# Two chunks of an MLP down-projection as seven block products in place of eight (Strassen), in a two-layer encoder on one core

## The chip, the cores and the metric

The kernel runs on one core of one Trainium2 chip. The metric is the device time of one execution, in microseconds (us): 2254.66 us, the median of 3 runs (2254.27 to 2255.26). The engines are named as in the profile: PE (matmuls), PEld (PE's weight loads), DVE (VectorE), ACT (ScalarE), POOL (GpSimd) and SP, whose queue starts the weight loads.

## The reference, cut to what matters

Two layers, each an attention mixer and a gated MLP, all in float32, with 256 tokens, a model width of 2048 and an MLP width of 5632:

```
def conv_ffn(h, w_up, conv_w, conv_b, w_down):
    u = h @ w_up                      # 256 x 2048 by 2048 x 11264
    u = depthwise conv of width 3 over positions, + conv_b
    gate, val = jnp.split(u, 2, axis=-1)
    return (jax.nn.silu(gate) * val) @ w_down     # 256 x 5632 by 5632 x 2048
...
for i in range(2):
    h = h + mixer_i(rms_norm(h, mix_norm[i]))     # grouped-query attention, then dilated windows
    h = h + conv_ffn(rms_norm(h, ffn_norm[i]), w_up[i], ...)
return rms_norm(h, final_norm)
```

## The kernel before

**Matmuls in three parts.** PE multiplies in a rounded float32 form, so every operand is split into a rounded high part and the rest. A product is three matmuls into one PSUM bank: high by high, high by low, low by high (lines 115 to 117).

**A feed.** `feed` (line 97) takes one chunk of 512 rows of a weight matrix and one block of 512 columns. SP loads it in two pieces of 128 x 1024 (512 KB each) into `raw` buffers, of which there are 4 (NRAW). ACT writes the high part `wh` (line 127), DVE the low part `wl` (line 128); there are 4 buffers of each (NHL). Both are issued under a priority that is raised by AHEAD = 60 instructions. PE then runs 24 matmuls: 2 token blocks (m) x 4 row blocks (kt) x 3. Two banks, `accs[0]` and `accs[1]`, hold the 128 + 128 tokens by 512 columns.

**Order.** The program is written out in Python and placed by a scheduler that takes, on each engine, the instruction with the best priority whose inputs and buffers are there. Side work is written as generators: `pending` ones move by one piece at every odd row block of a feed, `beside` ones at every even one, and `drain` writes out all that is left. A piece's place in the text gives its priority; it may run earlier when it is ready.

**The MLP.** `ffn` (line 362) runs in two halves of the MLP width: 6 chunks, then 5 (HALVES). In each half the up-projection makes a gate block and a value block per chunk; each is evacuated by ACT with the row scale (`stg`, line 359), turned by DVE and POOL (`turned`, lines 401 to 407, 16 POOL copies into a tile `u`), convolved by ACT (line 388) and DVE (line 396), and gate and value are multiplied on POOL (line 422). `act_split` (line 436) rounds the product into the left operands of the down-projection (`slots`, the tiles `a`). These steps run one or two chunks behind PE. After the last chunk, `flush` does the rest beside the first feeds of the down-projection.

**The down-projection.** It multiplies the half's chunks with `w_down`, in four column blocks n = 0 to 3, and adds to the residual `h`. Columns 0 and 1 run together (`project2`): all chunks but the last for n = 0, the same for n = 1, and then the last chunk, which is ready last, for both. Columns 2 and 3 follow one by one (`project`; the very last by `project_last`, which ends with the final norm and the output). `done` adds a finished block to `h`, two DVE operations of 128 x 512 (line 331 or 487). In the second half of layer 0 it also starts the transposes for the next mixer; in the second half of layer 1 it squares on ACT (line 488) and multiplies by the final gain on POOL (line 489).

PSUM has eight banks: four of tag `acc` for the projections, four of tag `ps` for everything else.

## Time and profile before

| what | value |
|---|---|
| median of 3 runs | 2254.66 us (2254.27 to 2255.26) |
| span of the profiled execution, first to last instruction | 2253.4 us |
| own time of the profiled execution | not given apart from its span; the runs' median is 1.3 us more |
| matmuls, weight loads | 10089 each |
| busy: PE, DVE, ACT, POOL | 2240.8, 1605.8, 1216.2, 760.4 us |
| wl splits of 128 x 1024 on DVE | 788, mean 1.27 us |
| wh splits of 128 x 1024 on ACT | 788, mean 1.06 us |
| moved by DMA | 439.56 MB, 195 GB/s |

A line of the profile names the source line, engine and operation, the tile written and the tiles read with their shape, and how often it ran; then the busy time with the mean of one in ns, and the idle time of the engine just before with what ended it. Lines in order of time begin with the start and the length in us; a bracket at the end holds the idle time ahead of the instruction and who ended it. Matmuls overlap each other, so that their lengths do not add up. Windows give, for a stretch of the span, its length, the busy time of PE, PEld, DVE, ACT and POOL with the number of instructions, the granted clock, and DMA's share and rate.

### The profile page before, as it was taken

What the parts mean: (1) busy time and instruction counts of PE and PEld (TensorE: products, weight loads), DVE (VectorE), ACT (ScalarE), POOL (GpSimd) and SP (SyncE); (2) the same over time, 40 slices, a digit from 0 to 9 for tenths busy, and PEclk for the clock granted to TensorE, in tenths of its full rate; (3) what the DMA queues carried; (4) which work ended last, traced back from release to release, by engine and by line L of the source; (5) the groups of instructions that cost most, each with busy time, mean ns of one, the idle gap of its engine ahead of it and who ended that gap; (6) DMA issues with size and microseconds to landing.
All of it is one profiled execution on the core that took longest, in us unless ns stands there. A gap on an engine that the chain in (4) does not pass through costs nothing.

```text
span 2253.4 us, 28552 instructions
## 1 busy us (share of the span) xinstructions
PE 2240.8 (99%) x10089; PEld 1860.1 (83%) x10089; DVE 1605.8 (71%) x2137; ACT 1216.2 (54%) x1691; POOL 760.4 (34%) x999
## 2 busy tenths in 40 slices
PE   9999999999999999999999999999999999999998
PEld 7888888888888888888888888888888888888887
DVE  6877967776546777878876877676777764576765
ACT  7676556555345655555454554445655543465653
POOL 2342165663006554010052007002665600256530
PEclk9999999999999999999999999999999999999999
DMA  8565665655555565565566555566555555555554
GB/s 302 191 222 172 203 201 190 195 193 195 194 193 192 194 193 188 191 215 195 184 191 195 180 187 175 180 201 211 195 193 193 193 196 192 193 195 194 191 196 150
DMA packets 125871, 439.56 MB, mean 195 GB/s; under 512 B 14232, under 2 KB 18072, under 8 KB 125600
## 3 DMA queue, kind: packets, MB, share of 16 engines
q1 hardware_dynamic: 123056, 429.05, 57.0%
q0 software_dynamic: 2384, 8.39, 1.5%
q8 instruction: 79, 1.29, 0.2%
q14 instruction: 64, 0.52, 0.1%
q10 hardware_dynamic: 288, 0.30, 0.0%
HBM read 432.34 MB, written 5.34 MB: 194 GB/s over the span
## 4 chain that ended last, share of the span: by engine, by line
PE 96%; DVE 2%; DMA 1%; issue 1%; POOL 1%; ACT 0%; SPq 0%; DVEq 0%; POOLq 0%; ACTq 0%
PE acc L116 31%; PE acc L115 31%; PE acc L117 31%; DVE wl L128 1%; DMA raw<-in_w_b_dram 1%; DVE tT L268 1%; PE ps L225 0%; PE ps L224 0%; PE ps L223 0%; PE ps L1031 0%; PE ps L221 0%; DMA raw<-in_w_a_dram 0%; ACT wh L127 0%; POOL wide L263 0%; POOL t L704 0%
## 5 line engine op out<-in xcount | busy, mean ns | idle before, releaser
L128 DVE TENSOR_TENSOR wl<-raw,wh 128x1024 fp32r<-128x1024 f32 (+1 forms) x804 | 1010.0, 1260 | 521.2 <-ACT wh L127 518.1
L127 ACT ACTIVATE wh<-raw 128x1024 fp32r<-128x1024 f32 (+1 forms) x804 | 840.8, 1050 | 800.7 <-PE acc L117 714.8
L115 PE MATMUL acc<-wh,xh 128*128 128x512 f32 x2176 | 848.7, 390 | 0.7 <-ACT wh L127 0.7
L116 PE MATMUL acc<-wl,xh 128*128 128x512 f32 x2176 | 847.6, 390 | 0.3 <-DVE wl L128 0.2
L117 PE MATMUL acc<-wh,xh 128*128 128x512 f32 x2176 | 847.3, 389 | 0.0
L406 POOL COPY u<-quad 32x256 f32<-32x256 f32 x704 | 489.4, 695 | 539.9 <-DVE quad L259 512.1
L117 PEld LDWEIGHTS acc<-wh,xh 128*128 128x128 f32 x2176 | 408.6, 188 | 85.5
L115 PEld LDWEIGHTS acc<-wh,xh 128*128 128x128 f32 x2176 | 408.8, 188 | 84.8 <-ACT wh L127 1.1
L116 PEld LDWEIGHTS acc<-wl,xh 128*128 128x128 f32 x2176 | 408.8, 188 | 84.5 <-DVE wl L128 1.4
L115 PE MATMUL acc<-wh,a 128*128 128x512 f32 x1008 | 392.8, 390 | 0.0
L116 PE MATMUL acc<-wl,a 128*128 128x512 f32 x1008 | 392.3, 389 | 0.0
L117 PE MATMUL acc<-wh,a 128*128 128x512 f32 x1008 | 392.2, 389 | 0.0
L117 PEld LDWEIGHTS acc<-wh,a 128*128 128x128 f32 x1008 | 189.2, 188 | 39.5 <-DVE a L210 0.2
L116 PEld LDWEIGHTS acc<-wl,a 128*128 128x128 f32 x1008 | 189.3, 188 | 39.0
L115 PEld LDWEIGHTS acc<-wh,a 128*128 128x128 f32 x1008 | 189.3, 188 | 38.6
L263 POOL COPY wide<-quad 32x256 f32<-32x256 f32 x165 | 107.2, 650 | 170.1 <-DVE quad L259 162.9
L422 POOL TENSOR_TENSOR cv<-cg,cv 128x1024 f32<-128x1024 f32 x22 | 71.1, 3232 | 135.7 <-DVE cv L396 135.7
L359 ACT ACTIVATE stg<-acc,rstd 128x512 f32<-128x512 f32 x122 | 82.9, 685 | 31.7 <-PE acc L117 31.7
L396 DVE SCALAR_TENSOR_TENSOR cg<-u,cw,cg 128x256 f32<-128x256 f32 x176 | 82.3, 511 | 4.5 <-ACT cg L388 4.5
L396 DVE SCALAR_TENSOR_TENSOR cv<-u,cw,cv 128x256 f32<-128x256 f32 x176 | 74.3, 479 | 15.5 <-ACT cv L388 15.3
L259 DVE STREAM_TRANSPOSE quad<-stg 128x512 f32<-128x512 f32 x88 | 59.4, 699 | 10.3 <-ACT stg L359 10.3
L268 DVE STREAM_TRANSPOSE tT<-h 32x256 f32<-32x256 f32 x144 | 62.8, 436 | 2.7
(172 smaller groups left out, 1037.0 us busy)
## 6 DMA issues: line engine op xcount, KB each, us to landing
raw<-in_w_up_dram SPq DMA_DIRECT2D x352, 512.0 KB, 4.5
raw<-in_w_down_dram SPq DMA_DIRECT2D x176, 512.0 KB, 4.2
raw<-in_w_b_dram SPq DMA_DIRECT2D x144, 512.0 KB, 4.4
raw<-in_w_bo_dram SPq DMA_DIRECT2D x48, 512.0 KB, 3.7
raw<-in_w_a_dram SPq DMA_DIRECT2D x40, 512.0 KB, 4.7
raw<-in_w_ao_dram SPq DMA_DIRECT2D x32, 512.0 KB, 4.0
raw<-in_w_a_dram SPq DMA_DIRECT2D x16, 256.0 KB, 5.8
there<-quad POOLq DMA_DIRECT2D x6, 512.0 KB, 3.2
```

Of the source, the lines that this page charges most:

```text
L115: nc.tensor.matmul(accs[m], xh[:, c], wh[:, j, :], start=st, stop=False)
L116: nc.tensor.matmul(accs[m], xh[:, c], wl[:, j, :], start=False, stop=False)
L117: nc.tensor.matmul(accs[m], xl[:, c], wh[:, j, :], start=False, stop=sp)
L127: nc.scalar.activation(wh[:, c], r[:, c], AF.Copy)
L128: nc.vector.tensor_tensor(wl[:, c], r[:, c], wh[:, c].bitcast(F32), ALU.subtract)
L259: nc.vector.transpose(quad[:, :, at, :], src.rearrange("p (x c t) -> p c x t", c=4, t=32))
L263: nc.gpsimd.tensor_copy(o[32 * c:32 * c + 32, :, 32 * q:32 * q + 32], quad[32 * q:32 * q + 32, c])
L268: nc.vector.transpose(o[cols].rearrange("p a (m t) -> p a m t", m=2)[:, :, :, rows], s[rows].rearrange("p m (a c) -> p a m c", c=P)[:, :, ...
L359: nc.scalar.activation(o[:, m, :], accs[m], AF.Copy, scale=rstd[:, m:m + 1])
L396: nc.vector.scalar_tensor_tensor(cj, halves(flat[:, j, o:o + NT])[:, ::-1], tap(n, j, i), cj, ALU.mult, ALU.add)
L406: nc.gpsimd.tensor_copy(u[32 * c:32 * c + 32, :, :, 32 * q:32 * q + 32], quad[32 * q:32 * q + 32, c].rearrange("p (j m) t -> p j m t", m=2))
L422: made.append(nc.gpsimd.tensor_tensor(cv, cg, cv, ALU.mult).ins)
```

## The change

In three of the four halves (both of layer 1, the first of layer 0) chunks 2 and 3 of the down-projection become *fast units*. A fast unit takes one chunk and two column blocks at once, as a 2 x 2 by 2 x 2 block product: the left matrix is cut into 2 token blocks x 2 halves of the chunk's rows, the weights into 2 halves of the rows x 2 column blocks. It makes seven block products in place of eight, each 2 row blocks x 3 matmuls, into seven banks; with the banks of the plain chunks eight are in use (`fast_accs`).

- `fast_unit` loads the four weight blocks b11, b12, b21, b22 (128 x 1024 each). DVE makes the four sums t1, b12, t2, t4, three of them in the tiles `u` and one in place, at a priority raised by 120. All seven right operands are split by ACT and DVE as in a feed.
- `combined` takes the place of `act_split` for these chunks: four differences of left blocks on DVE, and splits of those and of the blocks that are used as they are.
- `fold` adds the shared products to `h` after a pair's last fast unit: one ACT copy and eight DVE operations of 128 x 512, in four pieces beside the feeds.
- `pair` runs two column blocks together in a written order of plain feeds and fast units, in place of `project2` and `project`. Ahead of a fast unit it writes out all pending work.
- The last value block of a half is turned by ACT in place of POOL, and its product with the gate is made by DVE in place of POOL, in all four halves.
- Two more `raw` buffers come from the MLP's own pool: every third load takes one of them.
- Some tiles move: the final gain is loaded in four pieces into the tiles of the up-projection's operands, the bias lines use tiles of the left operands, the transposes use `cg` and `cv`, and a constant that nothing read is gone.

The order of the chunks, with f2 and f3 for the fast units and a plain chunk once for each of its two columns: in first halves 0 0 1 1 f2 4 4 f3 5 5 for columns 0-1 and 0 0 f2 1 1 f3 4 4 5 5 for columns 2-3; in the second half of layer 1 0 0 1 f2 1 f3 4 4, and 0 f2 1 f3 4 for columns 2-3 (the plain chunks of column 3 follow in `project_last`).

The core of the diff (left out: the moves of tiles to other tags, the bias lines and the gain's pieces):

```diff
-    def feed(accs, lhs, kg, wap, first, last, by_m=False, pieces=1, mid=None):
+    extra, count = [None], [0]
+
+    def raw_tile():
+        count[0] += 1
+        if extra[0] and count[0] % 3 == 0:
+            return extra[0].tile([P, 2, 512], F32, tag="raw2", name=nm("raw"), bufs=2)
+        return spool.tile([P, 2, 512], F32, tag="raw", name=nm("raw"), bufs=NRAW)
+
+    def feed(accs, lhs, kg, wap, first, last, by_m=False, pieces=1, mid=None, begun=()):
...
         raws, w = [], 2048 // pieces
         for i in range(max(pieces, 2)):
             if pieces < 4 or i % 2 == 0:
-                raws.append(spool.tile([P, 2, 512], F32, tag="raw", name=nm("raw"), bufs=NRAW))
+                raws.append(raw_tile())
             w = min(w, 1024)
             r = raws[-1].rearrange("p a c -> p (a c)")
...
                 c = slice(m * P, (m + 1) * P)
                 nc.tensor.matmul(accs[m], xh[:, c], wh[:, j, :], start=st, stop=False)
...
+            def u_tile(i):
+                return fp.tile([P, 4 * 2 * 129], F32, tag=f"u{i}", name=nm("u"))
+
+            us = []
+
+            def new_us():
+                us[:] = [u_tile(i).rearrange("p (j m t) -> p j m t", j=4, m=2) for i in range(3)]
+                for u in us:
+                    nc.gpsimd.memset(u[:, :, 0, P:], 0.0)
+
 
...
-            def turned(s, u):
+            def turned(s, u, by_act=0):
                 quad = quad_tile(fp, "quad", 2)
                 for m in range(2):
                     quad_T(quad, slice(m, 8, 2), s[:, m])
-                for q, c in QC:
-                    nc.gpsimd.tensor_copy(u[32 * c:32 * c + 32, :, :, 32 * q:32 * q + 32],
-                                          quad[32 * q:32 * q + 32, c].rearrange("p (j m) t -> p j m t", m=2))
+                for i, (q, c) in enumerate(QC):
+                    o = u[32 * c:32 * c + 32, :, :, 32 * q:32 * q + 32]
+                    src = quad[32 * q:32 * q + 32, c].rearrange("p (j m) t -> p j m t", m=2)
+                    if i < 16 - by_act:
+                        nc.gpsimd.tensor_copy(o, src)
+                    else:
+                        nc.scalar.activation(o, src, AF.Copy)
 
...
-            def product(value):
+            def product(value, eng=nc.gpsimd):
                 n, u, cv, cg, made, _, _ = value
                 yield from conv((n, u, cv))
-                made.append(nc.gpsimd.tensor_tensor(cv, cg, cv, ALU.mult).ins)
+                made.append(eng.tensor_tensor(cv, cg, cv, ALU.mult).ins)
...
+                turned(s, blk[1], 16 if blk[0] - NPAIR in (HALVES[0][1] - 1, NPAIR - 1) else 0)
                 for _ in range(1 if last else 4):
                     yield
                 yield from conv(gate)
...
             def act_split(value):
                 slots, k0 = value[5:]
                 cv = value[2]
+                if k0 // 4 in fast:
+                    slots[-1 - k0 // 4] = combined(cv, k0)
+                    ready.add(k0 // 4)
+                    yield
+                    return
                 for j in range(4):
                     hi, lo = slots[k0 + j]
                     tc.keep_in_program_order(nc.scalar.activation(hi, cv[:, j, :], AF.Copy))
                     nc.vector.tensor_tensor(lo, cv[:, j, :], hi.bitcast(F32), ALU.subtract)
                     if j == 1:
                         yield
+                ready.add(k0 // 4)
+
+            def combined(cv, k0):
+                v = cv.rearrange("p (b j) (m t) -> p b j m t", b=2, m=2)
+                st = fp.tile([P, 4, 2, P], F32, tag="st", name=nm("st"))
+                a11, a21, a12, a22 = v[:, 0, :, 0], v[:, 0, :, 1], v[:, 1, :, 0], v[:, 1, :, 1]
+                for o, x, y in ((0, a21, a22), (2, a21, a11), (1, a11, st[:, 0]), (3, a12, st[:, 1])):
+                    nc.vector.tensor_tensor(st[:, o], x, y, ALU.subtract)
+                own = [pair_slot(k0 + 2 * i, [P, 4, 2, P], F32R, "s") for i in range(2)]
+                sx = fp.tile([P, 6, 2, P], F32R, tag="sx", name=nm("sx"), bufs=2)
+                hA, lA, hB, lB = sx[:, 0:2], sx[:, 2:4], sx[:, 4], sx[:, 5]
+                split_in_order(*own, st)
+                split_in_order(hA, lA, v[:, :, :, 0])
+                split_in_order(hB, lB, a22)
+                pick = {1: (hA[:, 0], lA[:, 0]), 2: (hA[:, 1], lA[:, 1]), 4: (hB, lB)}
+                for q, i in ((5, 0), (6, 1), (7, 2), (3, 3)):
+                    pick[q] = own[0][:, i], own[1][:, i]
+                return pick
+
+            def fast_unit(acc, pick, wap0, wap1, begun, end):
+                def load(wap, i):
+                    r = raw_tile()
+                    nc.sync.dma_start(r.rearrange("p a c -> p (a c)"), wap[:, i * 1024:(i + 1) * 1024])
+                    return r
+
+                def new_sum(i, x, y):
+                    t = u_tile(i)[:, :1024].rearrange("p (a c) -> p a c", a=2)
+                    nc.vector.tensor_tensor(t, x, y, ALU.add)
+                    return t
+
+                b11, b12, b21, b22 = load(wap0, 0), load(wap1, 0), load(wap0, 1), load(wap1, 1)
+                with tc.high_priority(offset=2 * AHEAD):
+                    t1 = new_sum(0, b11, b12)
+                    nc.vector.tensor_tensor(b12, b12, b22, ALU.add)
+                    t2 = new_sum(1, b11, b12)
+                    t4 = new_sum(2, t2, b21)
+                for i, (q, r) in enumerate(((1, b11), (2, b21), (3, b22), (5, t1), (7, b12), (6, t2), (4, t4))):
+                    wh = spool.tile([P, 2, 512], F32R, tag="wh", name=nm("wh"), bufs=NHL)
+                    wl = spool.tile([P, 2, 512], F32R, tag="wl", name=nm("wl"), bufs=NHL)
+                    with tc.high_priority(offset=AHEAD):
+                        nc.scalar.activation(wh, r, AF.Copy)
+                        nc.vector.tensor_tensor(wl, r, wh.bitcast(F32), ALU.subtract)
+                    xh, xl = pick[q]
+                    for j in range(2):
+                        st = q not in begun and j == 0
+                        sp = q in end and j == 1
+                        nc.tensor.matmul(acc[q], xh[:, j], wh[:, j], start=st, stop=False)
+                        nc.tensor.matmul(acc[q], xh[:, j], wl[:, j], start=False, stop=False)
+                        nc.tensor.matmul(acc[q], xl[:, j], wh[:, j], start=False, stop=sp)
+                    begun.add(q)
+                    step(i % 2 == 0)
+
+            def fold(acc, n0, n1):
+                def hs(m, n):
+                    return h[:, m, n * 512:(n + 1) * 512]
+
+                tt = nc.vector.tensor_tensor
+                one, two = (fp.tile([P, 2, 512], F32, tag="quad", name=nm("fold"), bufs=2) for _ in range(2))
+                a, v, w, c = one[:, 0], one[:, 1], two[:, 0], two[:, 1]
+                nc.scalar.activation(a, acc[1], AF.Copy)
+                tt(v, acc[6], a, ALU.subtract)
+                tt(w, acc[7], v, ALU.add)
+                yield
+                tt(c, acc[5], v, ALU.add)
+                tt(v, acc[5], w, ALU.add)
+                yield
+                tt(hs(0, n0), hs(0, n0), a, ALU.add)
+                tt(hs(0, n1), hs(0, n1), c, ALU.add)
+                yield
+                tt(hs(1, n0), hs(1, n0), w, ALU.subtract)
+                tt(hs(1, n1), hs(1, n1), v, ALU.add)
+
+            def fast_accs():
+                (a3, a8), (a2, a4) = new_acc(), new_acc()
+                acc = {q: ps_tile() for q in (1, 5, 6, 7)}
+                acc.update({2: a2, 3: a3, 4: a4, 8: a8})
+                return acc
+
+            def pair(wd, ns, lhs, order, done):
+                while beside:
+                    step(True)
+                acc, begun = fast_accs(), set()
+                sides = [acc[2], acc[4]], [acc[3], acc[8]]
+                fasts = [kg for kg, side in order if side is None]
+                for i, (kg, side) in enumerate(order):
+                    if side is None or kg == order[-1][0]:
+                        drain()
+                    while kg not in ready:
+                        step()
+                    if side is None:
+                        later = {s for _, s in order[i + 1:]}
+                        end = [q for q, s in ((1, None), (5, None), (6, None), (7, None), (2, 0), (4, 0), (3, 1))
+                               if not later & {None, s}]
+                        fast_unit(acc, lhs[-1 - kg], wd[ns[0], kg], wd[ns[1], kg], begun, end)
+                        if kg == fasts[-1]:
+                            beside.append(fold(acc, *ns))
+                        continue
+                    mine = ((2, 4), (3, 8))[side]
+                    end = not any(s == side for _, s in order[i + 1:])
+                    feed(sides[side], lhs, kg, wd[ns[side], kg], not begun.issuperset(mine), end,
+                         begun=[m for m in range(2) if mine[m] in begun])
+                    begun.update(mine)
+                    if end:
+                        done(sides[side], ns[side])
+                return acc
...
                 yield
-                yield from product(value)
+                yield from product(value, nc.vector)
                 yield
...
@@ -455,8 +589,12 @@
                 return us[0]
 
             kgs = list(range(4))
+            ready = set()
             for hf, (p0, p1) in enumerate(HALVES):
                 slots = {}
+                ready.clear()
+                new_us()
+                fast = (2, 3) if hf == 0 or last else ()
                 last_value = None
                 for p in range(p0, p1):
                     k0 = 4 * (p - p0)
...
@@ -556,13 +694,30 @@
 
                 np_ = p1 - p0
                 wd = w_down[l][:, p0:p1]
-                done(project2(wd, 0, 1, slots, list(range(np_)), 1, lambda a: done(a, 0)), 1)
-                for n in (2, 3):
-                    if last and hf == 1 and n == 3:
-                        project_last(wd, n, slots, list(range(np_)), first_out, last_out)
-                    else:
-                        done(project(wd, n, slots, list(range(np_))), n)
+                extra[0] = fp
+                if last and hf == 1:
+                    load_fin()
+                rest = [kg for kg in range(np_) if kg not in fast]
+                both = {kg: [(kg, 0), (kg, 1)] for kg in rest}
+                if not fast:
+                    done(project2(wd, 0, 1, slots, rest, 1, lambda a: done(a, 0)), 1)
+                    for n in (2, 3):
+                        done(project(wd, n, slots, rest), n)
+                    continue
+                f0, f1 = ([(kg, None)] for kg in fast)
+                if hf == 0:
+                    pair(wd, (0, 1), slots, both[0] + both[1] + f0 + both[4] + f1 + both[5], done)
+                    pair(wd, (2, 3), slots, both[0] + f0 + both[1] + f1 + both[4] + both[5], done)
+                    continue
+                pair(wd, (0, 1), slots, both[0] + [(1, 0)] + f0 + [(1, 1)] + f1 + both[4], done)
+                acc = pair(wd, (2, 3), slots, [(0, 0)] + f0 + [(1, 0)] + f1 + [(4, 0)], done)
+                while beside:
+                    step(True)
+                hs = h[:, 0, 1536:]
+                nc.vector.tensor_tensor(hs, acc[3], hs, ALU.add)
+                project_last(wd, 3, slots, rest, first_out, last_out)
             assert not spare
+            extra[0] = None
         return hTn, ss
 
```

More of the change, by code (lines that the diff above doesn't have):

```diff
@@ L112, in mms @@
                 xh, xl = lhs[4 * kg + kt][:2]
-                st, sp = first and kt == 0, last and kt == 3
+                st, sp = first and kt == 0 and m not in begun, last and kt == 3
                 c = slice(m * P, (m + 1) * P)
@@ L154, in project_last @@
             for i in range(2):
-                raw, wh, wl = (spool.tile([P, 2, 512], dt, tag=t, name=nm(t), bufs=b)
-                               for t, dt, b in (("raw", F32, NRAW), ("wh", F32R, NHL), ("wl", F32R, NHL)))
+                raw = raw_tile()
+                wh, wl = (spool.tile([P, 2, 512], F32R, tag=t, name=nm(t), bufs=NHL) for t in ("wh", "wl"))
                 nc.sync.dma_start(raw.rearrange("p a c -> p (a c)"), w[n, kg][:, i * 1024:(i + 1) * 1024])
@@ L364, in ffn @@
             junk = junk_of(fp)
-            next_space[0] = fp, ("quad", 2), ("tT", 1)
+            next_space[0] = fp, ("quad", 2), ("cv", 1)
             drain(1)
@@ L370, in ffn, with fin, load_fin @@
             hTn, ss = {}, new_ss()
-            if last:
-                fin = fp.tile([P, D], F32, name="fin")
-                nc.gpsimd.dma_start(fin, final_norm.partition_broadcast(P))
+            fins = []
+            def fin(c0, c1):
+                return fins[c0 // 512][:, c0 % 512:(c1 - 1) % 512 + 1]
+            def load_fin():
+                for n in range(4):
+                    fins.append(hpool.tile([P, 512], F32, tag=f"x{n}", name=nm("fin")))
+                    nc.gpsimd.dma_start(fins[n], final_norm[n * 512:(n + 1) * 512].partition_broadcast(P))
             def tap(n, j, i):
@@ L376, in tap @@
                 return cw[:, k:k + 1]
-            us = [fp.tile([P, 4, 2, 129], F32, name=nm("u")) for _ in range(3)]
-            for u in us:
-                nc.gpsimd.memset(u[:, :, 0, P:], 0.0)
+            def u_tile(i):
[5 more added lines that the diff above has]
+                    nc.gpsimd.memset(u[:, :, 0, P:], 0.0)
             def halves(v):
```

54 lines of the change are left out of this document (24 added, 30 removed).

## The prediction

> **What bounds the kernel now.** I read the page first (busy shares, then the chain that ended last), then the waits of PE, and then one down-projection in order of time.
>
> ```profile
> span 2253.4 us, 28552 instructions
> PE 2240.8 (99%) x10089; PEld 1860.1 (83%) x10089; DVE 1605.8 (71%) x2137; ACT 1216.2 (54%) x1691; POOL 760.4 (34%) x999
> PE 96%; DVE 2%; DMA 1%; issue 1%; POOL 1%; ACT 0%; SPq 0%; DVEq 0%; POOLq 0%; ACTq 0%
> L116 PE MATMUL acc<-wl,xh 128*128 128x512 f32 x2176 | 847.6, 390 | 0.3 <-DVE wl L128 0.2
> ...
> PE acc L115 <- ACT wh L127: 0.7, 1, 0.7
> PE acc L116 <- DVE wl L128: 0.2, 1, 0.2
> ```
>
> The page's lines say that PE carries the end; the last two, from the waits of PE, say that the splits of the weights (wh by ACT, wl by DVE) were late by 0.9 us in the whole run. So fewer matmuls shorten the kernel as long as the splits stay in time. What a matmul is worth is not the 390 ns of the row, which is its length in a pipeline: 3 x 2176 + 3 x 1008 of them at 390 ns would be 3.7 ms. Two starts in order of time give the pitch:
>
> ```profile
> 545.81 0.39 PE L115 MATMUL acc<-wh,a 128*128 128x512 f32 x1
> 551.25 0.39 PE L115 MATMUL acc<-wh,a 128*128 128x512 f32 x1
> ```
>
> One feed (a chunk of 512 rows against 512 columns, 24 matmuls) lies between them: 5.44 us, 0.2267 us a matmul. The stages concerned, as windows (columns: length, PE, PEld, DVE, ACT and POOL busy, clock, DMA share, GB/s); the first two are the first half of layer 0, the last two the second half of layer 1, each as columns 0-1 and columns 2-3:
>
> ```profile
> 518.80:584.10 65.30, 65.30 (x289) 54.07 (x288) 42.64 (x49) 31.71 (x40) 13.93 (x17) 1.00 0.57 194
> 584.10:649.40 65.30, 65.30 (x290) 54.08 (x289) 31.84 (x29) 25.47 (x24) 0.00 (x0) 1.00 0.56 193
> 2136.20:2190.60 54.40, 54.40 (x242) 45.06 (x241) 37.69 (x45) 28.85 (x40) 16.89 (x19) 1.00 0.59 194
> 2190.60:2240.00 49.40, 49.40 (x220) 40.92 (x219) 27.14 (x24) 20.83 (x25) 6.22 (x5) 1.00 0.47 154
> ```
>
> DVE is free for 23, 33, 17 and 22 us in them. That is what the change spends.
>
> **What it saves.** A fast unit (one chunk, two column blocks) is 7 products of 2 x 3 matmuls: 42 in place of 48. Three halves have 2 chunks x 2 pairs of columns each: 12 units, 72 matmuls, 72 x 0.2267 = 16.3 us. A unit lasts 42 x 0.2267 = 9.52 us.
>
> **What it costs on DVE.** All rows are from the second half of layer 1, down-projection, in order of time:
>
> ```profile
> 2146.23 1.22 DVE L128 TENSOR_TENSOR wl<-raw,wh 128x1024 fp32r<-128x1024 f32 x1 [0.21 <-ACT wh L127]
> 2150.60 2.17 DVE L396 SCALAR_TENSOR_TENSOR cv<-u,cw,cv 128x256 f32<-128x256 f32 x5 [3.15 <-ACT cv L388]
> 2153.03 1.23 DVE L128 TENSOR_TENSOR wl<-raw,wh 128x1024 fp32r<-128x1024 f32 x1 [0.26 <-ACT wh L127]
> 2154.17 1.40 DVE L396 SCALAR_TENSOR_TENSOR cv<-u,cw,cv 128x256 f32<-128x256 f32 x3
> 2155.48 4.55 DVE L128 TENSOR_TENSOR wl<-raw,wh 128x1024 fp32r<-128x1024 f32 x2
> 2159.96 0.74 DVE L442 TENSOR_TENSOR a<-cv,a 128x256 fp32r<-128x256 f32 x2
> 2161.84 0.75 DVE L442 TENSOR_TENSOR a<-cv,a 128x256 fp32r<-128x256 f32 x2
> 2162.51 2.35 DVE L128 TENSOR_TENSOR wl<-raw,wh 128x1024 fp32r<-128x1024 f32 x2
> 2167.94 1.23 DVE L128 TENSOR_TENSOR wl<-raw,wh 128x1024 fp32r<-128x1024 f32 x1 [1.49 <-ACT wh L127]
> 2185.40 1.28 DVE L487 TENSOR_TENSOR h<-acc,h 128x512 f32<-128x512 f32 x2
> 2195.14 2.37 DVE L128 TENSOR_TENSOR wl<-raw,wh 128x1024 fp32r<-128x1024 f32 x1 [1.12 <-ACT wh L127]
> ```
>
> A full wl takes 1.23 us, but the next operation starts 1.14 us after it (2153.03 to 2154.17); 1.14 is the price of every two-input 128x1024 operation here, the sums and the product too. A unit needs 4 sums (4.56) and 7 wl (7.98): 12.5 us of DVE against 9.52 of PE. A slow feed needs 2 wl, 2.28 against 5.44. So a unit is short by 3.0 us and each slow feed beside it gives 3.2 back: the sums must be done ahead, in the slow feeds. The fold is 8 operations of 128x512, like the two at 2185.40 (0.64 each): 5.1 us a pair, beside the adds that stay.
>
> How late may a wl be? Its buffer (4 of them) comes free when a half-feed ends, and it is ready 2.6 us later, 5.6 us ahead of its use. Inside a unit a buffer serves 1.36 us, so the seventh wl is due 6 x 1.36 = 8.16 us after the unit starts. I set DVE's work up to there against that time.
>
> *First unit, first half (both layers).* The value block's turn, convolution and product (the flush) lie right ahead of it.
>
> ```profile
> 519.29 0.39 PE L115 MATMUL acc<-wh,a 128*128 128x512 f32 x1
> 528.79 1.22 DVE L128 TENSOR_TENSOR wl<-raw,wh 128x1024 fp32r<-128x1024 f32 x1 [0.20 <-ACT wh L127]
> 533.16 2.17 DVE L396 SCALAR_TENSOR_TENSOR cv<-u,cw,cv 128x256 f32<-128x256 f32 x5 [3.15 <-ACT cv L388]
> 2136.72 0.39 PE L115 MATMUL acc<-wh,a 128*128 128x512 f32 x1
> 2138.59 11.34 POOL L406 COPY u<-quad 32x256 f32<-32x256 f32 x16 [9.96 <-DVE quad L259]
> 2155.74 3.22 POOL L422 TENSOR_TENSOR cv<-cg,cv 128x1024 f32<-128x1024 f32 x1 [5.81 <-DVE cv L396]
> L297 ACT ACTIVATE wide<-quad 32x256 f32<-32x256 f32 x18 | 7.5, 415 | 1.0 <-DVE tot L323 0.8
> ```
>
> Four slow feeds from 519.29: the unit starts at 541.05, its seventh wl is due at 549.2. DVE is clear at 530.0. Left to do: 8 wl (9.1), the convolution (2.17 + 1.40), the product, now DVE's (1.14), the last rounding (0.74 + 0.75), the sums (4.6): 19.9, that is 549.9, and up to 2 us more where DVE waits for the turned block. The turn goes from POOL (11.34) to ACT: 16 x 0.415 = 6.6, with two or three wh of 1.06 between, so between 3 us earlier and no earlier. Late by 0 (the rounding left for later) to 2.8; I take 1 for each of the two.
>
> *First unit, second half of layer 1.* Only three slow feeds: start 2153.0, due 2161.2. DVE is clear at 2147.5. Left: 6 wl (6.8), 3.6, 1.14, 1.5, 4.6, and the block differences of the chunk before (4 x 0.37 + 1.14 + 0.64 + 0.37 in place of 1.5: 2.1 more): 19.7, to 2167.2. Late by 4.5 (rounding left) to 7; I take 5.5.
>
> *First unit of columns 2-3.* From one seventh wl to the next. First halves: 4 wl, fold 5.1, 4 adds 2.6, 4 wl, sums and 7 wl: 29.3 against 1.36 + 4 x 5.44 + 8.16 = 31.3, nothing. Second half of layer 1, with one chunk fewer: 27.0 against 25.8, late by 1.2, and POOL's gain products sit there as now: the row at 2195.14 (2.37 for 1.23) and its like cost 1.9. 0 to 3.1, I take 2.
>
> *The other six units.* First halves 17.1 of DVE against 20.4; second half of layer 1 14.8 against 15.0. Nothing; the cover there is 3.3 and 0.2 us.
>
> *What the trace does not show.* The pair holds all eight PSUM banks. At three starts it may wait for the value block's evacuation, at two the next up-projection for the last adds (1.28, row 2185.40); ahead of a start:
>
> ```profile
> 2136.24 1.37 ACT L359 ACTIVATE stg<-acc,rstd 128x512 f32<-128x512 f32 x2
> raw<-in_w_down_dram SPq DMA_DIRECT2D x176, 512.0 KB, 4.2
> 10.00:20.00 10.00, 10.00 (x46) 8.15 (x46) 9.50 (x18) 9.05 (x18) 1.29 (x2) 1.00 1.03 388
> ```
>
> So 0 to 6.7 in all; a gain is excluded, for PE waits nothing there now. I take one wait, 1.4, since a buffer pair that was freed a feed earlier is there each time. The loads: a unit takes four of 0.52 MB, 5.4 us at the 388 GB/s of the third line; six raw buffers let the fourth start when the wl of two feeds back is done, some 14 us ahead. I take nothing; the bound is one late DVE operation a unit, 12 x 1.23 = 14.8, priced below. The block differences of the other five fast chunks run in the up-projections; nothing there waits for them. The bias lines, gains and buffers that move tag are needed tens of us later: nothing.
>
> Sum: -16.3 + 2 + 5.5 + 2 + 1.4 = -5.4 us. The median is 2254.66, 1.3 above the profiled span; both move alike: 2249.3.
>
> **Two rules of the Trainium skill.** The collision row first: while POOL's product ran (2155.74 to 2158.96) two wl took 4.55 in place of 2.35. "SBUF — State Buffer", Who interferes with whom, says that a DVE instruction with two SBUF inputs contends with a GpSimd instruction that reads SBUF, one waiting for all of the other. The trace agrees; by this rule the product moved to DVE costs 1.14 and gives back 2.2, which the ledgers hold already, as they price every wl at its undisturbed 1.14. The second speaks against the change. The warm-up's matmuls ran slower than all later ones:
>
> ```profile
> L319 PE MATMUL ps<-warm 128*128 128x512 f32 x11 | 5.1, 643 | 1.5 <-DVE warm L316 1.5
> ```
>
> 643 ns, where 390 is usual. "TensorE: Matmul & The Clock Gate", Part 1, has the array fall back to half clock after an idle window of about 3.4 us. By it the 5.5 us stall, if it came in one piece, would cost up to 3.4 us at half speed, an estimate from that page of 1.7 us more. No row of the stages shows such a fall (clock 1.00), and a stall shared among seven products would not be such a window.
>
> **The rivals.** *The sums stand at the head of DVE's queue (slower).* DVE runs in order. A sum that is placed early and waits for the unit's fourth load (4.2 us to land) holds every wl behind it, and inside a unit a wl has only 1.5 us to spare (3 x 1.36 less the 2.6). For it: DVE has no slack in the second half of layer 1 (14.8 of 15.0). Against it: the 14 us of lead worked out above. At one operation (1.23) a unit it adds 14.8: -5.4 + 14.8 = +9.4, 2264. It decides from 0.8 us a unit on (10 us in all). *Cancelled (no change).* All the PSUM waits come, 6.7, and the stalls at 9.5: -0.1, 2254.6. *All hidden (faster).* The scheduler finds a place for all of it, as it did for the flush so far: -16.3, 2238.4; with the stall of the second half of layer 1 alone, -10.8, 2243.9. Against it: 6 us of DVE work too many there. *It doesn't do what it says:* excluded, the count of matmuls falls by what is written out.
>
> **How the numbers follow.** My forecast -5.4, with its own bounds -12 to +1: 0.38. All hidden: 0.17. Cancelled: 0.13. The queue: 0.32. Within 0.2% (4.5 us, about what a measurement of this kernel tells from none) fall the cancelled case and a little of the forecast's upper part. Faster 0.51, same 0.15, slower 0.34. The range leaves out a tenth at each end: below 2241 only nearly everything hidden, above 2265 the queue at more than one operation a unit.
>
> **What would show it.** PE instructions fall by 72 to 10017; DVE's count rises by 48 sums, 36 wl and 48 fold operations, its busy time by about 150 us. PE waits for wl at the first unit of the second half of layer 1, 4 to 7 us, and about 1 us at those of the first halves; units of columns 2-3 in first halves run at 9.5 us. Waits of PE on DMA, or on the sums, at most units would be the rival; waits of acc on an evacuation or an add, the PSUM bound. I am wrong if DVE is late in units whose ledger has room.

## The result: slower by 0.7%

The changed kernel takes 2271.32 us (median of 5 runs, 2269.46 to 2271.44), the kernel before 2254.66: 16.7 us more, ratio 1.0071 (95% interval 1.0059 to 1.0083). 2249.3 was forecast, with a range to 2265. The page of the changed kernel, the lines that answer to those of before:

```profile
span 2269.6 us, 28639 instructions
PE 2237.2 (99%) x10017; PEld 1848.8 (81%) x10017; DVE 1728.1 (76%) x2292; ACT 1286.3 (57%) x1791; POOL 717.4 (32%) x939
PE 87%; DVE 5%; DMA 2%; POOL 2%; issue 2%; ACT 1%; SPq 0%; DVEq 0%; POOLq 0%; ACTq 0%
```

The 72 matmuls are gone (10089 to 10017), yet the chain of waits runs over PE for 87% of the span in place of 96%. PE's busy share still reads 99%: matmuls of 390 ns started every 227 ns hide every stop shorter than the difference, and slow matmuls count as busy. The waits of PE say more (us in all, times, the longest; the five largest, without two of about 2 and 1.5 us that both kernels have ahead of other work):

```profile
PE ps L521 <- DVE wl L515: 4.7, 4, 1.8
PE acc L121 <- DVE h L337: 3.7, 2, 2.0
PE ps L520 <- ACT wh L514: 3.6, 3, 2.3
PE acc L121 <- DVE h L625: 3.5, 1, 3.5
PE acc L122 <- DVE wl L134: 3.2, 4, 1.5
```

Lines 514 and 515 are wh and wl of a fast unit, 520 to 522 its matmuls; 337 and 625 are the adds of a finished column block to `h`. In the kernel before the longest wait for a split was 0.7 us, and there was none for an add. For the table I took the starts of PE in order of time and counted what each lies beyond 0.2267 us after the one ahead of it, where that is more than 0.02 us; the row on the pace of the units has what is smaller:

| place | layer 0, first half | layer 1, first half | layer 1, second half |
|---|---|---|---|
| saved (24 matmuls each) | 5.4 | 5.4 | 5.4 |
| lost at the first unit and the feed after it | 4.5 | 4.4 | 8.7 |
| lost at the start of columns 2-3 | 3.8 | 1.9 | 6.4 |
| lost later | 0 | 0.2 | 1.2 |
| lost in the pace of four units | 0.7 | 0.7 | 0.7 |
| net | +3.6 | +1.8 | +11.6 |

From the first matmul of a stage to its last, the three stages are 3.7, 1.9 and 11.6 us longer than before, together 17.2; the rest of the program is 0.9 us shorter, and the span grew by 16.2.

**The pace of a unit.** The last row of losses needs no stop. A unit's first matmul, and the first one of the feed behind it, where PE waited for nothing:

```profile
566.68 0.40 PE L520 MATMUL ps<-wh,sx 128*128 128x512 f32 x1
576.35 0.39 PE L121 MATMUL acc<-wh,a 128*128 128x512 f32 x1
```

That is 9.67 us for 42 matmuls where 42 x 0.2267 is 9.52, and 0.03 us more come in the feed behind: 0.17 a unit, 2.0 for the twelve. In the first three and the last of a unit's products the starts lie 0.228 to 0.236 us apart, in the others 0.227; why was not traced.

**The start of columns 2-3**, second half of layer 1: PE, and DVE in order of time (lines left out at the dots):

```profile
2206.13 0.79 PE L121 MATMUL acc<-wh,a 128*128 128x512 f32 x1 [3.54 <-DVE h L625]
2206.72 0.63 PE L122 MATMUL acc<-wl,a 128*128 128x512 f32 x1
2207.15 0.63 PE L123 MATMUL acc<-wh,a 128*128 128x512 f32 x1
...
2195.38 1.23 DVE L501 TENSOR_TENSOR u<-raw,raw 128x1024 f32<-128x1024 f32 x1 [0.26 <-DMA raw<-in_w_down_dram]
...
2197.72 0.68 DVE L543 TENSOR_TENSOR h<-h,fold 128x512 f32<-128x512 f32 x1
2199.11 1.23 DVE L507 TENSOR_TENSOR raw<-raw,raw 128x1024 f32<-128x1024 f32 x1 [0.70 <-DMA raw<-in_w_down_dram]
2200.25 0.69 DVE L544 TENSOR_TENSOR h<-h,fold 128x512 f32<-128x512 f32 x1
2200.85 1.22 DVE L501 TENSOR_TENSOR u<-raw,raw 128x1024 f32<-128x1024 f32 x1
2201.99 1.22 DVE L134 TENSOR_TENSOR wl<-raw,wh 128x1024 fp32r<-128x1024 f32 x1
2203.12 1.22 DVE L501 TENSOR_TENSOR u<-u,raw 128x1024 f32<-128x1024 f32 x1
2204.26 1.22 DVE L134 TENSOR_TENSOR wl<-raw,wh 128x1024 fp32r<-128x1024 f32 x1
2205.39 1.28 DVE L625 TENSOR_TENSOR h<-acc,h 128x512 f32<-128x512 f32 x2
```

Column 0's last feed is the one ahead of the last plain feed (2196.75 to 2202.4), so its banks were complete at about 2197.0, and the fold's last operation on that column (line 543) was done at 2198.4. The two adds that free the banks start at 2205.39, 7 us later. Ahead of them DVE stands idle for 0.70 us until the load of a sum lands, and does three of the four sums of the *next* unit (lines 501 and 507), two wl and an operation of the fold. PE's wait ends at the first add.

The same place in the first half of layer 0:

```profile
589.40 0.47 PE L121 MATMUL acc<-wh,a 128*128 128x512 f32 x1 [1.98 <-DVE h L337]
...
584.55 1.23 DVE L501 TENSOR_TENSOR u<-raw,raw 128x1024 f32<-128x1024 f32 x1 [1.32 <-DMA raw<-in_w_down_dram]
585.69 0.69 DVE L544 TENSOR_TENSOR h<-h,fold 128x512 f32<-128x512 f32 x1
586.29 2.35 DVE L134 TENSOR_TENSOR wl<-raw,wh 128x1024 fp32r<-128x1024 f32 x2
588.56 1.28 DVE L337 TENSOR_TENSOR h<-acc,h 128x512 f32<-128x512 f32 x2
```

Column 0 was complete at about 582.0. One sum stands ahead of the adds here, and DVE is idle for 1.32 us for its load while the adds could run: 2.5 us together, more than the stop. Layer 1's first half has the same picture, with 1.03 us of idle time.

**The first unit of that half**:

```profile
2167.87 0.50 PE L520 MATMUL ps<-wh,s 128*128 128x512 f32 x1 [2.31 <-ACT wh L514]
2170.13 0.50 PE L521 MATMUL ps<-wl,s 128*128 128x512 f32 x1 [1.75 <-DVE wl L515]
...
2149.42 1.22 DVE L507 TENSOR_TENSOR raw<-raw,raw 128x1024 f32<-128x1024 f32 x1
2152.38 1.22 DVE L134 TENSOR_TENSOR wl<-raw,wh 128x1024 fp32r<-128x1024 f32 x1 [1.74 <-ACT wh L133]
2164.01 1.40 DVE L416 SCALAR_TENSOR_TENSOR cv<-u,cw,cv 128x256 f32<-128x256 f32 x3
2165.44 1.23 DVE L501 TENSOR_TENSOR u<-raw,raw 128x1024 f32<-128x1024 f32 x1
2167.72 1.22 DVE L501 TENSOR_TENSOR u<-u,raw 128x1024 f32<-128x1024 f32 x1
```

t2 (2165.44) starts when the last convolution is done, because its tile is the `u` that the convolution still reads; at 2150 DVE stood idle for 1.74 us with t2's inputs there. PE waits for t2's splits.

**The clock.** Windows behind the two stops of the second half of layer 1 (the third figure from the end is the granted clock):

```profile
2170.00:2175.00 5.00, 4.87 (x14) 3.80 (x15) 4.84 (x6) 3.07 (x4) 0.00 (x0) 0.66 0.47 179
2205.00:2210.00 5.00, 3.87 (x9) 3.10 (x10) 5.00 (x7) 1.45 (x4) 3.03 (x1) 0.50 0.72 229
```

Slow matmuls start every 0.427 us and last 0.63 (2206.72 and 2207.15 above). Behind three stops (one in layer 0's first half, these two) this costs 1.7, 1.6 and 2.7 us: 6.0 of the 31 lost to stops and slow matmuls, counted in the table.

### The profile page after: what moved, and what is told of

The parts are those of the page before. It is cut to its first block, busy times and chain, and to the rows that moved or that the text cites. A ratio compares the mean times of both kernels' runs of the same rounds, so it can differ in the third digit from the quotient of the medians.

```text
span 2269.6 us, 28639 instructions
## 1 busy us (share of the span) xinstructions
PE 2237.2 (99%) x10017; PEld 1848.8 (81%) x10017; DVE 1728.1 (76%) x2292; ACT 1286.3 (57%) x1791; POOL 717.4 (32%) x939
## 4 chain that ended last, share of the span: by engine, by line
PE 87%; DVE 5%; DMA 2%; POOL 2%; issue 2%; ACT 1%; SPq 0%; DVEq 0%; POOLq 0%; ACTq 0%
PE acc L122 27%; PE acc L121 27%; PE acc L123 27%; DMA raw<-in_w_down_dram 2%; POOL wide L269 2%; DVE wl L515 1%; DVE wl L134 1%; DVE u L501 1%; DMA raw<-in_w_a_dram 1%; PE ps L522 0%; PE ps L521 0%; PE ps L520 0%; PE ps L231 0%; DVE cv L416 0%; PE ps L230 0%
## 5 line engine op out<-in xcount | busy, mean ns | idle before, releaser
L134 DVE TENSOR_TENSOR wl<-raw,wh 128x1024 fp32r<-128x1024 f32 (+1 forms) x756 | 939.7, 1250 | 393.3 <-ACT wh L133 389.0
L133 ACT ACTIVATE wh<-raw 128x1024 fp32r<-128x1024 f32 (+1 forms) x756 | 790.5, 1050 | 680.7 <-PE acc L123 604.0
L429 POOL COPY u<-quad 32x256 f32<-32x256 f32 x640 | 457.3, 715 | 331.5 <-DVE quad L265 306.3
L121 PE MATMUL acc<-wh,a 128*128 128x512 f32 x816 | 319.0, 393 | 7.2 <-DVE h L337 3.7
L122 PE MATMUL acc<-wl,a 128*128 128x512 f32 x816 | 319.9, 392 | 3.1 <-DVE wl L134 3.0
L123 PE MATMUL acc<-wh,a 128*128 128x512 f32 x816 | 319.2, 391 | 0.0
L121 PEld LDWEIGHTS acc<-wh,a 128*128 128x128 f32 x816 | 154.6, 189 | 40.6 <-ACT wh L133 4.5
L122 PEld LDWEIGHTS acc<-wl,a 128*128 128x128 f32 x816 | 154.2, 189 | 36.5 <-DVE wl L134 4.8
L123 PEld LDWEIGHTS acc<-wh,a 128*128 128x128 f32 x816 | 154.1, 189 | 32.3 <-DVE a L216 0.2
L446 POOL TENSOR_TENSOR cv<-cg,cv 128x1024 f32<-128x1024 f32 x18 | 57.9, 3215 | 108.3 <-DVE cv L416 108.3
L514 ACT ACTIVATE wh<-raw 128x1024 fp32r<-128x1024 f32 x48 | 50.6, 1058 | 56.2 <-PE acc L123 47.2
```

The lines of the kernel that those rows point to most:

```text
L121: nc.tensor.matmul(accs[m], xh[:, c], wh[:, j, :], start=st, stop=False)
L122: nc.tensor.matmul(accs[m], xh[:, c], wl[:, j, :], start=False, stop=False)
L123: nc.tensor.matmul(accs[m], xl[:, c], wh[:, j, :], start=False, stop=sp)
L133: nc.scalar.activation(wh[:, c], r[:, c], AF.Copy)
L134: nc.vector.tensor_tensor(wl[:, c], r[:, c], wh[:, c].bitcast(F32), ALU.subtract)
L429: nc.gpsimd.tensor_copy(o, src)
```

## The experiments

Theory after the trace: DVE serves the wrong work first (**order**: sums ahead of the adds that free banks; a sum's tile that is held too long). Rival: DVE has too much work there whatever the order (**load**). Each ratio is to the kernel before as it ran beside the experiment (2254.98 to 2255.28 us); the us lost come from the one execution that was traced.

**Adds first.**

```diff
                     if end:
-                        done(sides[side], ns[side])
+                        with tc.high_priority(offset=2 * AHEAD):
+                            done(sides[side], ns[side])
```

> Edit: in a pair, the adds of a finished column block get the same raised priority (120) as the sums. In the changed kernel PE lost 12.0 us at the three starts of columns 2-3 (3.9, 1.9 and 6.2, the matmuls at half clock behind the two longer stops included), waiting for these adds, which stood behind the sums and the fold on DVE. Theory 'order' (the adds come last although PE's banks hang on them): these stops go and nothing takes their place, 2259 to 2262 us. Rival 'load' (DVE has too much to do there, whatever the order): the stops come back at the next unit's wl, 2267 to 2271 us.

Measured: 2265.89 us, ratio to before 1.005 (1.0033 to 1.0067), between the two expectations; the traced execution is the fastest of four, 2263.72. The waits of PE show why; the two at line 337 are gone, the one of the second half of layer 1 (now line 626) is not:

```profile
PE acc L122 <- DVE wl L134: 4.7, 5, 1.9
PE acc L121 <- DVE h L626: 2.4, 1, 2.4
```

By starts of PE, the first halves lose nothing at columns 2-3 any more (3.8 and 1.9 in the changed kernel): there it was the order. The second half of layer 1 loses 7.2 there and in the two feeds behind (6.4 and 1.2 in the changed kernel), with 1.9 now waiting for a wl. But the edit moved only one of column 0's two adds there (other lines between are left out):

```profile
2190.73 0.68 DVE L626 TENSOR_TENSOR h<-acc,h 128x512 f32<-128x512 f32 x1
2193.06 2.31 DVE L507 TENSOR_TENSOR raw<-raw,raw 128x1024 f32<-128x1024 f32 x1
2195.90 1.21 DVE L501 TENSOR_TENSOR u<-raw,raw 128x1024 f32<-128x1024 f32 x1
2197.04 0.68 DVE L543 TENSOR_TENSOR h<-h,fold 128x512 f32<-128x512 f32 x1
2197.64 1.27 DVE L626 TENSOR_TENSOR h<-acc,h 128x512 f32<-128x512 f32 x2
...
2192.31 1.99 POOL L628 TENSOR_TENSOR h<-h,fin 128x512 f32<-128x512 f32 x1 [61.46 <-issue]
```

The other add changes the same part of `h` as the fold's operation of line 543, which is written ahead of it and was not raised; so it came right behind that, 7 us after the first one, with two sums between. One of them (line 507) took 2.31 us in place of 1.22 beside POOL's product with the gain, which the raised add had let start. So this run does not separate order from load in the second half of layer 1; raising the fold with the adds was not tried.

**No sums.**

```diff
-                with tc.high_priority(offset=2 * AHEAD):
-                    t1 = new_sum(0, b11, b12)
-                    nc.vector.tensor_tensor(b12, b12, b22, ALU.add)
-                    t2 = new_sum(1, b11, b12)
-                    t4 = new_sum(2, t2, b21)
+                t1, t2, t4 = b11, b11, b21
```

> Leaves out the four weight sums of each unit (the plain blocks are used in their place, so the products are other ones); loads, splits, matmuls and folds stay. Theory 'DVE' (the sums' time and their waits make PE stop): nearly all stops go, what is left is under 4 us, so 2240 to 2246 us, below the kernel before. Rival 'structure' (eight banks in use, seven splits and four loads a unit make PE stop by themselves): 2255 us or more.

Measured: 2242.38 us, ratio 0.9942 (0.9927 to 0.9957): 12.6 us under before, of 16.3 that the matmuls can save. In the three stages 0.7 us of stops are left; with the 2.0 us of the units' pace that accounts for 2.7 of the 3.7 us that are missing. The loads, the seven splits, the eight banks and the fold are all still there, so none of them stops PE by itself: it is the sums, their time and their waits on DVE, and what stands behind them.

**First halves only.**

```diff
-                fast = (2, 3) if hf == 0 or last else ()
+                fast = (2, 3) if hf == 0 else ()
...
```

> Fast units in the first halves of both layers only; the second half of layer 1 runs as in the kernel before (with its last value block turned by ACT and multiplied by DVE). Theory 'place' (16.3 us lost there against 5.4 saved): 10 to 11 us off the changed kernel, 2260 to 2262 us, still above the kernel before. Rival (the stops there come from a delay that is handed on from the first halves): under 5 us off, 2266 us or more.

Measured: 2259.47 us, ratio 1.0019 (1.001 to 1.0029): 11.9 us off the changed kernel, near what 'place' said. The second half of layer 1 loses by its own making, as the table has it (11.6).

**The late tile to the late sum.**

```diff
+                s1, s2, s4 = (1, 2, 0) if hf == 0 else (0, 2, 1)
                 with tc.high_priority(offset=2 * AHEAD):
-                    t1 = new_sum(0, b11, b12)
+                    t1 = new_sum(s1, b11, b12)
                     nc.vector.tensor_tensor(b12, b12, b22, ALU.add)
-                    t2 = new_sum(1, b11, b12)
-                    t4 = new_sum(2, t2, b21)
+                    t2 = new_sum(s2, b11, b12)
+                    t4 = new_sum(s4, t2, b21)
```

> The three sum tiles are the convolution's tiles u; the edit gives the one that the last value block still holds to the sum that is needed last (t4), in place of t1 (first halves) and t2 (second half of layer 1). Theory 'tile' (the first unit of a half stops because its sums wait for that tile): the stops there shrink from 4.5, 4.3 and 8.7 us to about half, 2262 to 2265 us. Rival 'load' (DVE is short of time there anyway): 2268 to 2271 us.

Measured: 2266.18 us, ratio 1.0047 (1.0032 to 1.0062), between the two expectations; the traced execution is the fastest of four, 2262.42, so that the gains read from it are those of a good one. The first units of the first halves, with the feed behind, lose 1.6 each in place of 4.5 and 4.4, the second half of layer 1 still 7.5 of 8.7. The tile was most of it in the first halves, a seventh in the last. Beside that, the start of columns 2-3 in layer 0 lost 1.9 in place of 3.8: the stop there was 1.60 us, not 1.98, and no slow matmuls followed.

**Both orders.** The two edits together:

> Both orders at once: the adds at raised priority and the late tile given to t4, three halves with fast units. By the stops seen with each alone (1.6 us in each first half with the tiles, no wait for adds there with the priority, about 14 us left in the second half of layer 1): 17 us of stops against 16.3 saved. Theory 'order in the first halves, load in the second half of layer 1': 2256 to 2260 us, still not faster than before. Rival 'order everywhere': under 2252 us.

Measured: 2260.23 us, ratio 1.0022 (1.0013 to 1.0032); 1.6, 2.1 and 13.9 us lost in the three halves. The two edits repair the first halves and leave the last one, where, as in the run with the adds first, one of column 0's adds still comes behind the fold and two sums.

**Both orders, first halves only** (the edits of adds first, of the late tile and of first halves only):

> The same two edits, with fast units in the first halves only: 48 matmuls fewer, 10.9 us, against 1.6 us of stops in each. Theory 'order in the first halves, load in the second half of layer 1': 2247 to 2249 us, faster than the kernel before by 6 to 8. Rival (the two edits bring new stops when they stand together): 2252 us or more.

Measured: 2251.04 us, ratio 0.998 (0.9971 to 0.9988): faster than before by 4.2 us, between the two expectations. The waits of PE for the units' splits are down to

```profile
PE ps L522 <- DVE wl L516: 2.5, 4, 0.8
PE acc L522 <- DVE wl L516: 0.3, 1, 0.3
```

and the stops in the two halves to 1.6 and 2.6. With 0.17 for the pace of each of the eight units, 5.3 of the 10.9 us are left, and from first matmul to last the two stages are in fact 3.1 and 2.1 us shorter than before. The traced execution (2249.93) lies 5.4 under the median of before, as this says; the median lies 4.2 under it. The runs of this kernel spread from 2248.68 to 2253.41, and the cause of that stays open.

**One chunk in the last half.** As the run before, and with it

```diff
-                fast = (2, 3) if hf == 0 else ()
+                fast = (2, 3) if hf == 0 else (2,) if last else ()
...
+                pair(wd, (0, 1), slots, both[0] + both[1] + f0 + both[3] + both[4], done)
+                acc = pair(wd, (2, 3), slots, [(0, 0), (1, 0)] + f0 + [(3, 0), (4, 0)], done)
```

> As the run with both edits in the first halves, and in the second half of layer 1 one fast chunk (2) in place of two, behind four plain feeds in columns 0-1 and two in columns 2-3: 60 matmuls fewer than before, 13.6 us, less 3.2 in the first halves. Theory 'load' for the second half of layer 1 (two units are more than DVE can carry there, one is not): 0 to 3 us of stops there, 2244 to 2248 us. Rival 'tail' (the stops there belong to that half whatever the number of units: gain products on POOL, adds, folds): 2250 us or more.

Measured: 2250.57 us, ratio 0.9978 (0.9969 to 0.9987): the time lies in the range of the rival 'tail', though the trace speaks against that rival. The last half now loses 2.4 us to stops, where it lost 13.9 with two chunks and both orders, so the stops do hang on the units; since the units also stand elsewhere and the fold has more feeds around it, this does not separate load from order. The two units save 2.7 us there, and the stage lasts 108.93 us against 108.83 before: one chunk in that half gains nothing. The forecast of 2244 to 2248 missed because the first halves lost 2.3 and 2.6 (3.2 in all was said) and the pace of ten units costs 1.7. The run cannot be told from the one before it.

**The sums on POOL.** `nc.gpsimd` in place of `nc.vector` for the four sums, in the changed kernel:

> The changed kernel with the four sums of a unit on POOL in place of DVE. DVE is relieved of 4.6 us a unit; POOL takes about 3.2 for each (its product of the same size in the profile before), and a wl that runs beside one took about twice its time there. Theory 'DVE': if only DVE's own work counted, 2246 to 2255 us. Rival 'port' (two-input operations of the two engines hold each other up, and a chain of four sums takes 13 us): 2268 to 2300 us. I hold the rival for likelier.

Measured: 2294.38 us, ratio 1.0173 (1.0154 to 1.0191). Groups by line and shape, first of the changed kernel, then of this run:

```profile
L515 DVE TENSOR_TENSOR wl<-raw,wh 128x1024 fp32r<-128x1024 f32 x48 | 58.1, 1220 | 9.9 <-ACT wh L514 9.9
L501 DVE TENSOR_TENSOR u<-raw,raw 128x1024 f32<-128x1024 f32 x24 | 29.3, 1221 | 7.8 <-DMA raw<-in_w_down_dram 7.6
L534 DVE TENSOR_TENSOR fold<-ps,fold 128x512 f32<-128x512 f32 x6 | 4.1, 684 | 0.0
```

```profile
L515 DVE TENSOR_TENSOR wl<-raw,wh 128x1024 fp32r<-128x1024 f32 x48 | 83.4, 1750 | 11.2 <-ACT wh L514 11.2
L501 POOL TENSOR_TENSOR u<-raw,raw 128x1024 f32<-128x1024 f32 x24 | 74.8, 3116 | 159.2 <-DVE cv L416 74.3 <-DMA raw<-in_w_down_dram 48.0 <-DVE fold L537 20.4
```

A wl of a unit takes 1750 ns in place of 1220, and a sum 3116 in place of 1221. Taking the sums off DVE slows what DVE keeps. The Trainium skill, "SBUF — State Buffer", Who interferes with whom, has such a collision of a DVE instruction with two SBUF inputs and a GpSimd one that reads SBUF, and the 48 wl of the group agree with it. How much of the 23 us over the changed kernel is this, and how much the longer chain of sums, was not separated.

**A stop by itself.** The kernel before, with chains of ScalarE copies written into PE's stream:

```diff
+            nc.tensor.matmul(a[:, :P], x, x, start=True, stop=True)
+            with tc.high_priority(offset=2 * AHEAD):
+                for i in range(k):
+                    nc.scalar.activation(t, t if i else a[:, :P], AF.Copy)
+            for acc in accs:
+                nc.tensor.matmul(acc[:, :P], t, x, start=True, stop=True)
```

> The kernel before with four stops of PE written into it, one ahead of the first feed of column 2 in each half: a matmul into a spare bank, a chain of 1, 3, 5 or 10 ScalarE copies of 128x128, and a matmul that waits for the chain and writes the two banks of the column, which the feed then overwrites. It measures by itself what a stop costs. By the copies' lengths the stops are about 1, 1.6, 2.2 and 3.8 us. Theory 'clock' (a stop of 2 us and more is followed by some microseconds at half clock, as behind three stops of the changed kernel): matmuls at twice their pitch behind the two longer stops, not behind the shorter ones, about 2 us lost behind each; 2254.9 + 8.6 + 4 = 2267 to 2268 us. Rival (a stop costs its own length, and the slow matmuls of the changed kernel had another cause): 2263 to 2264 us, no slow matmuls.

Measured: 2274.71 us, ratio 1.0089 (1.0059 to 1.0118). PE in order of time at the four stops, and the feed's second matmul behind the last:

```profile
585.99 0.44 PE L151 MATMUL acc<-a,stop 128*128 128x128 f32 x2 [1.14 <-ACT stop L149]
927.02 0.63 PE L151 MATMUL acc<-a,stop 128*128 128x128 f32 x2 [2.91 <-ACT stop L149]
1862.60 0.69 PE L151 MATMUL acc<-a,stop 128*128 128x128 f32 x2 [2.51 <-ACT stop L149]
2207.45 0.69 PE L151 MATMUL acc<-a,stop 128*128 128x128 f32 x2 [5.26 <-ACT stop L149]
2208.47 0.63 PE L116 MATMUL acc<-wl,a 128*128 128x512 f32 x1
```

The stops came out longer than meant (1.14, 2.91, 2.51, 5.26). Behind the first no matmul is slow; behind each of the other three five to seven are, and 1.3 to 1.5 us are lost beside the stop itself. So the theory holds for what follows a stop, at 1.4 us in place of 2. The total missed by 7 us: the stops are 3.2 longer than planned, and three and not two had a slow tail. Stops and tails make 16 of the 19.6 us over the kernel before; the rest, which the added matmuls must share, was not taken apart.

## Why the prediction was wrong

*The saving* was 72 matmuls as said, but not quite 16.3 us: "A unit lasts 42 x 0.2267 = 9.52 us" proved to be 9.67, and 0.03 in the feed behind, 2.0 us for the twelve. With the sums left out 12.6 us came out.

*The prices* held: a wl of a unit and a sum have 1220 and 1221 ns in the groups above and start 1.14 us apart (2200.85 to 2201.99 above); an operation of the fold has 684 ns. DVE's busy time grew by 122 us (150 was said).

*The PSUM term failed*, and it is the largest miss. It was 1.4 us, "since a buffer pair that was freed a feed earlier is there each time". Measured: 12.1 us at the three starts of columns 2-3, of which 4.4 are slow matmuls. The banks were complete a feed earlier, but not freed: the adds that free them stood on DVE behind sums that no matmul needed for another 10 us and more, and behind the waits of these sums for their loads. With the adds raised, the two stops of the first halves vanish. The prediction had named this sign, waits of acc on an add.

*The ledgers failed in their form.* They set DVE's whole work against the time at which the seventh wl is due, as if DVE did it in the order of need. That bounds a stop from below only. In the first halves they gave 1 us each and 4.5 and 4.4 came, most of it because a sum waited for a tile that the last convolution held; giving the tile to the last sum left 1.6, near the ledger. For the second half of layer 1 they gave 5.5 (4.5 to 7) and 8.7 came. Of that 1.6 are slow matmuls and 1.8 the feed behind the unit, and 1.2 went with the tile; that the other parts come near 5.5 may be luck. For the first unit of columns 2-3 of that half 1.2 us of overload were seen, but the stop came at the bank, in one piece of 3.5 us.

Together: 10.7 us more at the banks and 10.1 more at the first units (17.6 for 7.5). Either alone would have turned the forecast of -5.4 into a loss. The clock's 6.0 are inside both.

*The clock* was left out of the sum, for "a stall shared among seven products would not be such a window". The stalls were not shared: 1.98 and 3.54 came in one piece each, 2.31 and 1.75 in two. The rule that spoke against the change, in the Trainium skill's "TensorE: Matmul & The Clock Gate", Part 1, was right in kind. The estimate of 1.7 us that the prediction drew from it stands beside 1.6 to 2.7 measured, three times; the page speaks of an idle window of about 3.4 us, and here a stop of 1.98 was followed by slow matmuls.

*The rival "the sums stand at the head of DVE's queue"* came nearest. Its mechanism came too: at the three starts of columns 2-3 DVE was idle for 1.32, 1.03 and 0.70 us for the load of a sum, with adds behind it that could run. What the early sums held back there was the adds, not the splits, and at three places, not at every unit; that the rival's 2264 lies nearer the measured time than the forecast is in part luck.

## What to carry to other kernels

Where an engine off the critical path is to take on work, do not only add up its time against a due time: list for each of its queued operations who waits for it, and raise those that free the bottleneck's buffers above those that only prepare. Give a buffer that is still being read to the consumer that comes last. An operation that must come first carries what it hangs on with it: raising the adds alone left them behind the fold. And when an added stage is near the other engine's capacity, use it only where slack lies beside it: here two halves of three paid after repair (0.998), the third did not, with a repair that reached only a part of it.

## What the runs showed of the hardware

After the first 130 us of these kernels, no stop of PE of up to 1.74 us was followed by slow matmuls, unless a longer stop or slow matmuls lay right ahead of it. All stops of 2.5 us and more were. Between 1.87 and 2.4 us it went either way. The clearest case is one place near 144 us, which every run has, with a stop of 1.90 to 1.96 us; here in the kernel before, and in the run without sums:

```profile
143.74 0.39 PE L225 MATMUL ps<-kTh,qTl 128*128 128x256 f32 x1 [1.90 <-DVE qTl L210]
144.54 0.40 PE L116 MATMUL acc<-wl,xh 128*128 128x512 f32 x1
...
144.68 0.39 PE L231 MATMUL ps<-kTh,qTl 128*128 128x256 f32 x1 [1.96 <-DVE qTl L216]
145.51 0.63 PE L122 MATMUL acc<-wl,xh 128*128 128x512 f32 x1
```

In six of the eleven traced runs slow matmuls follow there, in five none (the kernel before and the changed one among these). A stop of 2.39 us in the run with the adds first had none behind it until PE stopped again. What decides in this range was not traced.

Where they came, in the changed kernel and in the run with the written stops, 5 to 12 matmuls started every 0.427 us in place of 0.227, which costs 1.3 to 2.7 us on top of the stop. At the start of columns 2-3 in layer 0 a stop of 1.98 us had them and one of 1.60 us had none: 1.9 us between the two.
